# A column group's modulation sum emitted later, and chunk A's mean placed by VectorE's clock

## The chip, the cores and the metric

The kernel runs on one core of a Trainium2 chip. The metric is the device time of one execution in microseconds (us). The core's engines are TensorE (PE in the profile: matmuls; PEld is its loading of weights), VectorE (DVE), ScalarE (ACT), GpSimd (POOL) and SyncE (SP, whose queue issues most transfers). Each engine works through its own program in order; semaphores hold an instruction back until what it reads is there.

## The reference

A trunk of two layers on a sequence of 1024 tokens with D = 1024 channels. Layer 0 mixes tokens by a causal Conformer convolution, layer 1 by a multi-scale pool; each is followed by a SwiGLU feed-forward of width 2816. Every sub-layer is an RMSNorm, then a shift and scale, the sub-layer, a gate and the residual add. Shift, scale and gate come from one conditioning vector c. What matters here is the modulation and layer 0's convolution:

```python
c_act = jax.nn.silu(c)
for i in range(DEPTH):
    mod = c_act @ ada_w[i] + ada_b[i]
    sh_m, sc_m, g_m, sh_f, sc_f, g_f = jnp.split(mod, N_ADA, axis=-1)
    h = modulate(rms_norm(x, norm_mix_g[i]), sh_m, sc_m)
    ...
    x = x + (1.0 + g_m)[:, None, :] * y
    h = modulate(rms_norm(x, norm_ffn_g[i]), sh_f, sc_f)
    y = swiglu_ffn(h, ffn_w_gate[i], ffn_w_up[i], ffn_w_down[i])
    x = x + (1.0 + g_f)[:, None, :] * y

def conformer_conv(h, w1, b1, w_dw, b_dw, ln_g, ln_b, w2, b2):
    u = h @ w1 + b1
    a, g = jnp.split(u, 2, axis=-1)
    u = a * jax.nn.sigmoid(g)
    u = causal_depthwise_conv(u, w_dw, width=31) + b_dw
    u = jax.nn.silu(layer_norm(u, ln_g, ln_b))
    return u @ w2 + b2
```

(`causal_depthwise_conv` stands for the long call of the convolution; `ada_w[i]` makes six groups of D columns, numbered 0 to 5 in the order of the split.)

## The kernel before

Channels lie on the 128 partitions, tokens along the free axis. The sequence is worked in two chunks of 512 tokens, A and B. D is cut into 8 blocks of 128 channels. Every product is made of three matmuls of 128 x 512 (`products`, L485), from the high and low halves of a weight and of an activation; the weights come from DRAM as f32 (`raw`) and are split into halves (`w`) on ScalarE and VectorE.

In layer 0 the names are these. `h` is the normed and modulated input, in a high and a low half for each block. `a` and `g` are the two halves of the pointwise product (`conv_in`, L713); u = (a + bias) times the sigmoid `t` of g. The depthwise convolution has 31 taps: VectorE adds up taps in `ca`, ScalarE and GpSimd share others as products `pr` that GpSimd adds up in `pa`, and for two of the blocks TensorE does all or part of them as `tap` products (`pe_taps`, L749). Then comes the layer norm over channels with silu (`layer_norm_silu`, L849): `acc`, the sum over the eight blocks, goes through a product with ones (`mean`), which is taken off u; the squares are added up and give `var`, VectorE takes its inverse root in small steps (`col`), and TensorE spreads it (`rstd`). Then u times rstd, silu on ScalarE, and the result `v` in two halves, which the products `y` (`conv_out`, L912) read. In layer 0's feed-forward the products are called `p`, then `dn`, which reads `g` again.

The columns of the modulation are made by `ada_columns` (L426), a generator: a load of 128 rows of `ada_w` (`adaw`), four small matmuls into `ada`, eight times for each group. `columns_done` (L449) then copies the sum out on ScalarE, waits a "spread", turns it into columns by small matmuls (`adac`), and adds the bias into `mod` on VectorE.

What sets the order: TensorE's program is written in the order in which the Python code emits its matmuls. All else, from norms to taps and modulation columns, is held in tasks, generators that are moved on between units of eight products by `pace` (L220). For that the code keeps a modelled clock of each engine (`clock`, with the keys PE, V, G and S), advanced by prices at every instruction that it emits (`Engine`, L104). A task says with each `yield` what it waits for, and `Task.step` (L250) turns this into a time `until` before which the task isn't moved on, measured against the modelled clock of TensorE. For an urgent task a word such as "stats" gives the clock at its last mark, plus the VectorE work emitted since, plus the fixed delay of `DELAY` (L66: 2.75 for "stats", 3.0 for "spread"). For others it gives the later of the clocks of VectorE and ScalarE, plus the delay. The order of VectorE, ScalarE and GpSimd then follows from a scheduler that takes the emitted instructions by priority.

`finish` (L232) forces given tasks to their end, with `until` left out of account, and moves the modelled clock of TensorE along with those of VectorE and GpSimd. In the main schedule it is called twice ahead of `ada_second`: for the first columns and for the taps of chunk A (L1589 and L1590).

Of the kernel before, what the change touches and what calls it, by code (L numbers as in the profile page):

```python
# [18 lines left out]
S = 1024  # L19
KT = D // P  # L20
# [3 lines left out]
CW = 31  # L24
# [28 lines left out]
PE_TAPS = {6: 15, 7: CW}  # L53
# [74 lines left out]
def trunk(ctx, tc, xT, c, vec, ada, adan, w1f, w1, wdg, w2, wgu, wdn, wpl, out):  # L128
    nc = tc.nc
    ctx.enter_context(tc.manual_schedule(engines={mybir.EngineType.PE}))  # L130
    clock = {"PE": 0.0, "V": 0.0, "G": 0.0, "S": 0.0}
# [9 lines left out]
    def matmul(out, lhsT, rhs, start, stop, more=False):  # L141
        n = out.shape[-1]
        clock["PE"] += n / 2400 * (1 if rhs.dtype == F32R else 4) + 0.0025
        last_mm[0] = nc.tensor.matmul(out, lhsT, rhs, start=start, stop=stop, skip_group_check=more).ins.name  # L144
# [47 lines left out]
    def nm(s):  # L192
        uid[0] += 1
        return f"{s}_{uid[0]}"
# [5 lines left out]
    forced = [False]  # L200
# [3 lines left out]
    def step(t, e):  # L204
        behind[0] = not t.urgent
        before = {k: engines[k].spent for k in "VG"}
        with tc.high_priority(offset=0 if t.urgent else -LATER):
            moved = t.step(e)
        behind[0] = False
        if V_.spent > before["V"] and getattr(t, "dots", False):  # L210
            recent.append(V_.last.ins)
            del recent[:-RECENT]
        if V_.spent > before["V"] and isinstance(t, Taps) and t.ch.i:
            beside.append(V_.last.ins)
            del beside[:-BESIDE]
        for k in "VG":
            clock[k] += (stretch[0] - 1) * (engines[k].spent - before[k])
        return moved
# [10 lines left out]
                if clock[e] < clock["PE"] + ahead:  # L229
                    moved = any(step(t, e) for t in list(tasks)) or moved  # L230

    def finish(*these):  # L232
        forced[0] = True
        for t in these:
            while not t.done:
                e = "V" if clock["V"] <= clock["G"] else "G"
                o = "VG"[e == "V"]
                if not any(step(q, e) for q in [t] + tasks) and not any(step(q, o) for q in [t] + tasks):
                    raise RuntimeError("nothing moves")
                clock["PE"] = max(clock["PE"], min(clock["V"], clock["G"]))  # L240
        forced[0] = False

    class Task:

# [5 lines left out]
        def step(self, e):  # L250
            if e != "V" or self.done or clock["PE"] < self.until and not forced[0]:
                return False
            try:
                if self.mark is None:
                    self.mark = clock["PE"] - V_.spent
                said = next(self.gen)
                if said == "wait":
                    return False
                if said in LOAD:
                    self.until = clock["PE"] + LOAD[said]  # L260
                elif said == "root":
                    self.until, self.mark = clock["PE"] + DELAY[said], None
                elif said is not None:
                    self.until = (self.mark + V_.spent if self.urgent else max(clock["V"], clock["S"])) + (DELAY if self.urgent or not lax[0] else DELAY_BEHIND)[said]
                    self.mark = None
            except StopIteration:
                self.done = True
                tasks.remove(self)
            return True
# [23 lines left out]
    def bank(name):  # L293
        return ps.tile([P, 512], F32, tag="mm", name=nm(name))
# [15 lines left out]
    def temp(n, name="t", bufs=0):  # L310
        t = tmp.tile([P, TMPW], F32, tag=name if bufs else "t", name=nm(name), bufs=bufs or 4)
        return t[:, :n]
# [46 lines left out]
    def V(name, j, n=1):  # L359
        b = _COLS[name] + j  # L360
        return vecs[:, b : b + n]
# [45 lines left out]
    def ada_gains(l, j, k, n, eng):  # L407
        b = (l * 6 + j) * KT + k
        m = mod[:, b : b + n]
        lk = l * KT + k  # L410
        if j in (1, 4):
            dst, g = (scale_m, "norm_mix_g") if j == 1 else (scale_f, "norm_ffn_g")
            dst = dst[:, lk : lk + n]
            eng.tensor_scalar(dst, m, 1.0, None, op0=ADD)
            eng.tensor_tensor(dst, dst, V(g, lk, n), op=MUL)
        elif j in (2, 5):
            dst = (gate_m if j == 2 else gate_f)[:, lk : lk + n]
            eng.tensor_scalar(dst, m, 1.0, None, op0=ADD)
            if j == 2 and l == 0:
                eng.tensor_tensor(gate_b, dst, V("conv_b2", k, n), op=MUL)  # L420
            if j == 2 and l % 2 == 1:
                eng.tensor_tensor(dst, dst, V("pool_ls", k, n), op=MUL)
# [26 lines left out]
    def columns_done(j, acc):  # L449

        rows = temp(Q)
        S_.copy(rows, acc[:, :Q])
        yield "spread"
        cols = bank("adac")
        for h in range(2):
            matmul(cols[:, 4 * h : 4 * h + 4], rows[:, h * P : h * P + P], quarters, start=True, stop=True)
        m = mod[:, j * KT : (j + 1) * KT]
        V_.tensor_tensor(m.rearrange("p (q h) -> p q h", h=2), cols[:, :KT].rearrange("p (h q) -> p q h", h=2),
                         V("ada_b", j * KT, KT).rearrange("p (q h) -> p q h", h=2), op=ADD)
        ada_gains(0, j, 0, KT, G_)  # L460
        ada_done.add((0, j))
# [186 lines left out]
    def unit(emit, *weights):  # L648
        units.append((weights, emit))
# [188 lines left out]
    def centred(vs, mean, n):  # L838

        held = temp(n, "ny", 2)  # L840
        S_.copy(held, mean)
        for k in range(KT):
            if k % 3 == 1:
                G_.tensor_tensor(vs[k], vs[k], held, op=SUB)
            else:
                V_.tensor_tensor(vs[k], vs[k], mean, op=SUB)
        yield

    def layer_norm_silu(ch):  # L849

        n = ch.n
        vs = [st["u", ch.i, k][:, HALO:] for k in range(KT)]
        acc = None
        for k in range(1, KT):
            while not (st["taps", ch.i][k - 1] and st["taps", ch.i][k]):
                yield "wait"
            was = vs[0] if k == 1 else acc
            if k == KT - 1 or ch.i and acc is None:
                acc = temp(n, "acc", 2)
            elif acc is None:  # L860
                acc = bank("acc")
            V_.tensor_tensor(acc, was, vs[k], op=ADD)
            yield
        if ch.i:
            calm[0], stretch[0] = True, 1.0
            clock["V"] = clock["G"] = clock["PE"]
        yield "soon" if ch.i else "stats"
        b = bank("mean")
        matmul(b, ones, acc, start=True, stop=True)
        if ch.i == 0:  # L870
            yield from centred(vs, b, n)
        else:
            for k in range(KT):
                V_.tensor_tensor(vs[k], vs[k], b, op=SUB)
                yield
        quiet[0] = not ch.i
        acc = yield from sum_sq([vs[k] for k in CENTRED], n)
        quiet[0] = False
        recent.clear()
        if ch.i == 0:  # L880
            for ins in beside:
                tc.add_manual_dep(ins, V_.last.ins.name, edge, reason="behind the sums")
            recent.extend(beside[2:])
            beside.clear()
        rstd = yield from mean_rsqrt(acc, n, when="settled" if ch.i else "stats", early=not ch.i)
        S_.activation(tmp.tile([P, 16], F32, tag="col0", name=nm("col"), bufs=1)[:, 0:1], acc[:, 0:1], AF.Silu)
        hv = [pair(f"h{ch.i}", "v") for _ in range(KT)]
        sws = []

        def low(k):  # L890
            (V_ if ch.i else (G_, V_)[k % 2]).tensor_tensor(hv[k][1], sws[k], hv[k][0].bitcast(F32), op=SUB)

        for k in range(KT):
            V_.tensor_tensor(vs[k], vs[k], rstd, op=MUL)
            sw = temp(n)
            sws.append(sw)
            S_.activation(sw, vs[k], AF.Silu, bias=V("conv_ln_b", k), scale=V("conv_ln_g", k))
            hi, lo = hv[k]
            if ch.i == 0 and k % 2 == 0:
                V_.tensor_copy(hi, sw)  # L900
            else:
                S_.copy(hi, sw)
            if ch.i == 0:
                low(k)
            elif k:
                low(k - 1)
            yield
        if ch.i:
            low(KT - 1)
        st["v", ch.i] = hv  # L910
# [623 lines left out]
    T = {}  # L1534
# [52 lines left out]
            unit(*u)  # L1587
    unit(lambda take: held.__setitem__(0, True))
    unit(lambda take: finish(T["ada", 0]))  # L1589
    unit(lambda take: finish(*(T["taps", 0, p] for p in range(KT) if PE_TAPS.get(p, 0) < CW)))  # L1590

    def ada_second(take):
        T["ada_f"] = Task(ada_columns((4, 5)), False, 0)
# [187 lines left out]
```

## Time and profile before

| | us |
|---|---|
| median of three runs | 1742.52 |
| the three runs | 1741.44, 1743.19, 1742.52 |
| the profiled execution, its own time | 1743.91 |
| its span | 1741.8 |
| idle time of DVE ahead of `x<-dn` in the span | 97.9 |
| granted clock of PE, mean | 0.994 |

The page of the profile gives the busy time of each engine, the chain of work that ended last (followed back from the last instruction), the groups of instructions by line, and the waits of an engine by what released it. A timeline row gives the start in us, the time of the run of instructions, the engine, the line, the operation, output<-inputs, shapes and count, and in brackets the idle time just ahead of it and what ended it. L122 is the line at which the helper issues every instruction of VectorE, ScalarE and GpSimd, and L144 that of every matmul, so rows are told apart by names. A row of the windows table gives the stretch, its length, TensorE's busy time and its instructions, TensorE's granted clock (1.00 is full), the DMA engines' busy share, and GB/s.

### The profile page before, as it was taken

Reading aid. Unit: us, or ns where it says so; the run is one execution under the profiler, and the core shown is the slowest. Engines: PE = TensorE matmul, PEld = TensorE weight load, DVE = VectorE, ACT = ScalarE, POOL = GpSimd, SP = SyncE. Lnnn points to the kernel's source line nnn. Section 1 sums busy time; section 2 is a strip of 40 time slices with the busy share of each in tenths; the row PEclk is TensorE's granted clock in tenths of the full one; section 3 lists DMA queues with packets and bytes.
Section 4 is the critical chain, followed back from the end, with each engine's and each line's share of the span. In section 5 each row is a group of like instructions: output and inputs, shape, how many; then the busy total and the mean of one; then the engine's idle time right before and its main releaser. Section 6 shows DMA issues by size and latency. Waiting matters only on the chain.

```text
span 1741.8 us, 21683 instructions
## 1 busy us (share of the span) xinstructions
PE 1705.0 (98%) x7746; PEld 1388.1 (80%) x7746; DVE 1305.9 (75%) x1878; ACT 788.9 (45%) x1080; POOL 465.9 (27%) x547
## 2 busy tenths in 40 slices
PE   6999999999998999999999999999999999999997
PEld 5777777778886888888888888888788888888887
DVE  8889898899668788877665987858767667555655
ACT  3669687876555233333223337457333333222213
POOL 4587767795001112221110201111111111000001
PEclk9999999999999999999999999999999999999999
DMA  7858987836776888877886837887777674656461
GB/s 286 289 168 224 228 230 201 213 100 208 242 236 183 268 257 266 279 245 253 319 271 214 265 114 221 238 294 209 231 216 208 174 217 139 265 199 208 165 237 61
DMA packets 111309, 384.91 MB, mean 221 GB/s; under 512 B 12129, under 2 KB 14305, under 8 KB 111202
## 3 DMA queue, kind: packets, MB, share of 16 engines
q1 hardware_dynamic: 74832, 256.11, 41.6%
q0 software_dynamic: 35280, 126.37, 29.3%
q8 instruction: 61, 1.00, 0.2%
q10 hardware_dynamic: 1090, 1.05, 0.2%
q14 instruction: 46, 0.38, 0.1%
HBM read 315.33 MB, written 63.96 MB: 218 GB/s over the span
## 4 chain that ended last, share of the span: by engine, by line
PE 87%; DVE 5%; DMA 3%; issue 2%; POOL 1%; ACT 1%; SPq 0%; DVEq 0%; POOLq 0%; ACTq 0%
PE dn L144 26%; PE a L144 22%; PE e L144 12%; PE p L144 11%; PE y L144 6%; PE g L144 3%; PE first L144 2%; PE tap L144 2%; DMA adaw<-in_adan_dram 1%; DMA gd<-g 1%; POOL pa L122 1%; PE ada L144 1%; DVE t L122 1%; PE var L144 1%; DVE adaw L122 1%
## 5 line engine op out<-in xcount | busy, mean ns | idle before, releaser
L122 ACT CAST w<-raw 128x1024 fp32r<-128x1024 f32 x269 | 281.7, 1050 | 489.4 <-PE dn L144 225.1
L144 PE MATMUL dn<-g,w 128*128 128x512 f32 (+1 forms) x2184 | 484.7, 383 | 2.1 <-DVE g L122 1.0
L144 PEld LDWEIGHTS dn<-g,w 128*128 128x128 f32 x2184 | 399.7, 188 | 82.6 <-DVE g L122 1.3
L122 DVE TENSOR_TENSOR w<-raw,w 128x1024 fp32r<-128x1024 f32 x195 | 241.7, 1243 | 63.7 <-ACT w L122 62.2
L144 PE MATMUL a<-n,w 128*128 128x512 f32 x1056 | 249.6, 392 | 4.0 <-DVE r L122 2.7
L144 PE MATMUL p<-h,w 128*128 128x512 f32 x1056 | 244.2, 390 | 0.9 <-DVE h L122 0.7
L144 PEld LDWEIGHTS a<-n,w 128*128 128x128 f32 x1056 | 198.9, 189 | 47.8 <-DVE r L122 3.7
L122 POOL TENSOR_TENSOR pa<-pa,pr 128x512 f32<-128x512 f32 x160 | 227.8, 1509 | 24.8 <-ACT pr L122 18.5
L144 PEld LDWEIGHTS p<-h,w 128*128 128x128 f32 x1056 | 197.3, 188 | 43.8 <-DVE h L122 1.5
L122 DVE SCALAR_TENSOR_TENSOR x<-dn,gains,x 128x512 f32<-128x512 f32 (+1 forms) x200 | 138.5, 725 | 98.1 <-PE dn L144 97.9
L122 DVE SCALAR_TENSOR_TENSOR ca<-u,vecs,ca 128x512 f32<-128x512 f32 x245 | 169.7, 745 | 0.5
L144 PE MATMUL a<-t,w 128*128 128x512 f32 x528 | 126.3, 395 | 3.9 <-ACT w L122 1.9
L144 PE MATMUL e<-b,w 128*128 128x512 f32 x528 | 123.4, 389 | 0.6 <-DVE r L122 0.6
L144 PE MATMUL e<-t,w 128*128 128x512 f32 x528 | 123.2, 389 | 0.0
L144 PEld LDWEIGHTS a<-t,w 128*128 128x128 f32 x528 | 100.5, 191 | 26.4 <-DVE w L122 3.1
L122 ACT ACTIVATE pr<-u,vecs 128x512 f32<-128x512 f32 x160 | 108.2, 716 | 25.1 <-POOL pa L122 17.9
L144 PEld LDWEIGHTS e<-b,w 128*128 128x128 f32 x528 | 99.0, 188 | 21.6 <-DVE r L122 1.0
L144 PEld LDWEIGHTS e<-t,w 128*128 128x128 f32 x528 | 99.1, 188 | 20.6
L1090 POOL DMA_DIRECT2D raw<-in_wgu_dram x42 | 37.2, 885 | 290.4 <-DMA raw<-in_wgu_dram 75.4
L161 POOL DMA_DIRECT2D gd<-g x76 | 46.3, 611 | 198.9 <-DVE g L122 198.5
L144 PE MATMUL y<-v,w 128*128 128x512 f32 x384 | 89.2, 391 | 0.5 <-DVE v L122 0.5
L144 PEld LDWEIGHTS y<-v,w 128*128 128x128 f32 x384 | 71.5, 188 | 17.5 <-issue 1.6
(164 smaller groups left out, 1982.9 us busy)
## 6 DMA issues: line engine op xcount, KB each, us to landing
raw<-in_wgu_dram SPq DMA_DIRECT2D x132, 512.0 KB, 4.8
raw<-in_wdn_dram SPq DMA_DIRECT2D x88, 512.0 KB, 7.0
gd<-g POOLq DMA_DIRECT2D x76, 512.0 KB, 6.9
g<-gd SPq DMA_DIRECT2D x76, 512.0 KB, 6.0
adaw<-in_ada_dram POOLq DMA_DIRECT2D x48, 512.0 KB, 7.0
raw<-in_wgu_dram POOLq DMA_DIRECT2D x42, 512.0 KB, 7.2
raw<-in_w_dram SPq DMA_DIRECT2D x36, 512.0 KB, 5.7
adaw<-in_adan_dram SPq DMA_DIRECT2D x32, 512.0 KB, 5.8
```

The source lines that it names most:

```text
L122: self.last = self.order(getattr(self.eng, name)(out, *args, **kw))
L144: last_mm[0] = nc.tensor.matmul(out, lhsT, rhs, start=start, stop=stop, skip_group_check=more).ins.name
L161: return order(nc.gpsimd.dma_start(*a))
L1090: d = order(nc.gpsimd.dma_start(w[i], wgu[l, fp, src], accum_op=ADD))
```

## The change

Three things change. `columns_done` yields a second "spread" between the adac matmuls and the add into `mod`. In `layer_norm_silu` chunk A's mean is placed by a new word, "mean": `until` becomes the later of the modelled clocks of VectorE and ScalarE, plus 1.0, where "stats" had added the VectorE work since the mark and 2.75. And the `finish` for the taps of chunk A puts the modelled clock of TensorE back to where it was.

```diff
-    def finish(*these):
-        forced[0] = True
+    def finish(*these, aside=False):
+        forced[0], was = True, clock["PE"]
...
                 clock["PE"] = max(clock["PE"], min(clock["V"], clock["G"]))
         forced[0] = False
+        if aside:
+            clock["PE"] = was
...
                     self.until = clock["PE"] + LOAD[said]
+                elif said == "mean":
+                    self.until, self.mark = max(clock["V"], clock["S"]) + 1.0, None
...
             matmul(cols[:, 4 * h : 4 * h + 4], rows[:, h * P : h * P + P], quarters, start=True, stop=True)
+        yield "spread"
         m = mod[:, j * KT : (j + 1) * KT]
...
-        yield "soon" if ch.i else "stats"
+        yield "soon" if ch.i else "mean"
...
-    unit(lambda take: finish(*(T["taps", 0, p] for p in range(KT) if PE_TAPS.get(p, 0) < CW)))
+    unit(lambda take: finish(*(T["taps", 0, p] for p in range(KT) if PE_TAPS.get(p, 0) < CW), aside=True))
```

TensorE's program differs only in its first 565 rows or so (up to some 430 us), with the same matmuls in another order; VectorE's, ScalarE's and GpSimd's differ further on only in the numbers of buffers. One tap product goes from VectorE to GpSimd's sum, and ScalarE loads its table of functions two times more.

The first place is TensorE's program at the mean of chunk A, where the units `a_1941`, `g_1942` and the next are products of chunk B with `h`. Before:

```order
L144 MATMUL a_1941<-h_774,w_1735 128x512 x3
L144 MATMUL ada_1976<-adaw_1930,ccols 32x256 x4
L144 MATMUL mean_1983<-acc_1928,ones 128x512
L144 MATMUL g_1942<-h_767,w_1795 128x512 x3
L144 MATMUL g_1942<-h_768,w_1795 128x512 x3
L144 MATMUL g_1942<-h_769,w_1795 128x512 x3
```

And with the change:

```order
L144 MATMUL a_1941<-h_774,w_1728 128x512 x3
L144 MATMUL ada_1976<-adaw_1930,ccols 32x256 x4
L144 MATMUL g_1942<-h_767,w_1794 128x512 x3
L144 MATMUL g_1942<-h_768,w_1794 128x512 x3
L144 MATMUL g_1942<-h_769,w_1794 128x512 x3
L144 MATMUL g_1942<-h_770,w_1794 128x512 x3
L144 MATMUL mean_2006<-acc_1928,ones 128x512
L144 MATMUL g_1942<-h_771,w_1794 128x512 x3
```

The mean stands four products, 12 matmuls, further back. The var and rstd rows that follow from it move by 12 matmuls each as well (from ahead of a unit to behind its fourth product), while the first row of `y` is the 305th of TensorE's program in both.

The second place is VectorE's program at the add into `mod` of the group j = 3, amid the taps of chunk A's block `u_687`. Before:

```order
L122 SCALAR_TENSOR_TENSOR ca_1557<-u_687,vecs,ca_1557 128x512
L122 TENSOR_TENSOR mod<-adac_1758,vecs 128x8
L122 SCALAR_TENSOR_TENSOR ca_1525<-u_687,vecs,ca_1525 128x512
L122 SCALAR_TENSOR_TENSOR ca_1557<-u_687,vecs,ca_1557 128x512
L122 SCALAR_TENSOR_TENSOR ca_1525<-u_687,vecs,ca_1525 128x512
L122 SCALAR_TENSOR_TENSOR ca_1557<-u_687,vecs,ca_1557 128x512 x3
L122 TENSOR_TENSOR ca_1525<-pa_1495,ca_1525 128x512
L122 SCALAR_TENSOR_TENSOR ca_1557<-u_687,vecs,ca_1557 128x512
```

And with the change:

```order
L122 SCALAR_TENSOR_TENSOR ca_1509<-u_687,vecs,ca_1509 128x512
L122 SCALAR_TENSOR_TENSOR ca_1571<-u_687,vecs,ca_1571 128x512 x2
L122 TENSOR_TENSOR ca_1509<-pa_1487,ca_1509 128x512
L122 SCALAR_TENSOR_TENSOR ca_1571<-u_687,vecs,ca_1571 128x512
L122 TENSOR_TENSOR mod<-adac_1779,vecs 128x8
L122 SCALAR_TENSOR_TENSOR u_687<-u_687,vecs,ca_1509 128x512
```

The add into `mod` has moved behind the sum with `pa` and behind six more taps of this block (the numbers of the buffers differ, the block is the same).

The third place is ScalarE's program ahead of the first silu of chunk A (the ACTIVATE that reads `u_638`, the first block). Before:

```order
L122 CAST w_2242<-raw_2240 128x1024
L122 ACTIVATE w_2242<-raw_2240 128x1024
L122 ACTIVATE t_2192<-u_638,vecs 128x512
L122 ACTIVATE t_2197<-u_638,vecs 128x512
L122 ACTIVATE t_2202<-u_649,vecs 128x512
```

And with the change:

```order
L122 CAST w_2197<-raw_2195 128x1024
L122 ACTIVATE w_2197<-raw_2195 128x1024
L122 ACT_TABLE_LOAD
L122 ACTIVATE t_2186<-g_2079,vecs 128x512
L122 ACT_TABLE_LOAD
L122 ACTIVATE t_2233<-u_638,vecs 128x512
L122 ACTIVATE t_2238<-u_638,vecs 128x512
```

A sigmoid (`t_2186`, of chunk B's unit `g_2079`) with a table load on either side now stands ahead of the silus; before, that sigmoid came behind all eight of them. On VectorE the u that reads it stands ahead of the products with rstd, with two taps behind it.

## The prediction

> **What bounds the kernel now.** I read the busy shares first, then the chain that ended last, then TensorE's waits, and then the timeline of the stretch that the change reorders.
>
> ```profile
> span 1741.8 us, 21683 instructions
> PE 1705.0 (98%) x7746; PEld 1388.1 (80%) x7746; DVE 1305.9 (75%) x1878; ACT 788.9 (45%) x1080; POOL 465.9 (27%) x547
> PE 87%; DVE 5%; DMA 3%; issue 2%; POOL 1%; ACT 1%; SPq 0%; DVEq 0%; POOLq 0%; ACTq 0%
> 460.43 43.52 PE y L144 x192
> ```
>
> TensorE is busy for 98% of the span and holds 87% of the chain. The chain's run of 192 matmuls in 43.52 us gives the price of one full matmul: 0.2267 us. The change neither adds nor removes a matmul, so it can only win or lose in TensorE's idle time and in its clock. TensorE runs in program order, and its order is the same again from about 430 us on. So the question is which waits before that point go, and which appear. By TensorE's waits and its timeline, these stand in the changed stretch:
>
> ```profile
> 173.04 0.64 PE L144 MATMUL ada<-adaw,ccols 128*32 128x256 f32 x8 [0.84 <-DMA adaw<-in_adan_dram]
> 246.18 5.29 PE L144 MATMUL y<-v,w 128*128 128x512 f32 x22
> 251.94 0.73 PE L144 MATMUL y<-v,w 128*128 128x512 f32 x2 [0.47 <-DVE v L122]
> 312.82 1.66 PE L144 MATMUL p<-h,w 128*128 128x512 f32 x6 [0.34 <-DVE h L122]
> 314.80 0.74 PE L144 MATMUL p<-h,w 128*128 128x512 f32 x2 [0.32 <-DVE h L122]
> 365.93 0.50 PE L144 MATMUL dn<-g,w 128*128 128x512 f32 x1 [0.44 <-ACT g L122]
> 367.41 13.65 PE L144 MATMUL dn<-g,w 128*128 128x512 f32 x59 [0.98 <-DVE g L122]
> ```
>
> Together 0.84 + 0.47 + 0.34 + 0.32 + 0.44 + 0.98 = 3.39 us. That is all that can be won by better placing: 0.19% of the span. A loss has no such lid.
>
> **The later modulation sum.** The add into `mod` held VectorE up once in this stretch:
>
> ```profile
> DVE mod L122 <- PE adac L144: 2.5, 1, 2.5
> 187.99 0.17 DVE L122 TENSOR_TENSOR mod<-adac,vecs 128x8 f32<-128x8 f32 x1 [2.55 <-PE adac L144]
> 209.63 1.50 DVE L122 TENSOR_TENSOR acc<-acc,u 128x512 f32<-128x512 f32 x2
> 212.36 1.13 PE L144 MATMUL mean<-acc,ones 128*128 128x512 f32 x2
> ```
>
> In the changed order six more tap instructions and a sum stand ahead of that add. The adac matmuls stand two rows later on TensorE, but the taps ahead of the add take about as long as the stall (six taps at 0.67 us and one sum, some 4.6 us), so the 2.55 us go. This pays nothing: chunk A's sum `acc` was ready at 209.63 + 1.50 = 211.13, before the mean's slot at 212.36. TensorE does not wait there now, and the mean's slot, not `acc`, starts the norm. If instead VectorE still stalled in full, the same 1.23 us of slack and the later slot would cover it up to 3.95 us. So 0, with bounds 0 to 0. The `ada` groups keep their number. Each is issued eight products (one unit) later than before or at a neighbouring place; two of them leave the y phase for the p phase, 0.57 us each from one phase to the other, 0 in the sum. Their loads on SyncE's queue keep the same issuing places as far as I can see. The wait of 0.84 us at 173.04 I leave as it is: bounds −0.84 (it vanishes) and +1.14, the longest wait of this kind, in a row quoted below; I take the one that the same place had.
>
> **The mean's place.** Before, the mean was issued ahead of a unit; now it stands after four products of it. Each product is three matmuls, so 12 × 0.2267 = 2.72 us later on TensorE. The variance and the rstd matmuls, each placed from the one ahead, stand 12 matmuls later too. The first y product stands in the same row of TensorE's order, with the same work ahead of it. So the path mean → centring → variance → rstd → silu → v starts 2.72 us later, and its end is where TensorE already waited 0.47 us, so there is no slack in front of it: v came at 251.89 and TensorE resumed at 251.94.
>
> What can shorten or lengthen this path is VectorE and ScalarE work between rstd and the last v:
>
> ```profile
> 228.49 5.35 DVE L122 SCALAR_TENSOR_TENSOR ca<-u,vecs,ca 128x512 f32<-128x512 f32 x8
> 234.01 4.87 DVE L122 TENSOR_TENSOR u<-u,rstd 128x512 f32<-128x512 f32 x8 [0.17 <-PE rstd L144]
> 248.57 2.72 DVE L122 SCALAR_TENSOR_TENSOR ca<-u,vecs,ca 128x512 f32<-128x512 f32 x4
> 251.21 0.68 DVE L122 TENSOR_TENSOR v<-t,v 128x512 fp32r<-128x512 f32 x1
> 224.64 0.67 ACT L122 ACTIVATE t<-g,vecs 128x512 f32<-128x512 f32 x1
> 225.32 1.28 ACT L122 ACT_TABLE_LOAD   x1
> 233.31 1.06 ACT L122 ACTIVATE w<-raw 128x1024 fp32r<-128x1024 f32 x1
> 234.80 2.23 ACT L122 ACTIVATE t<-u,vecs 128x512 f32<-128x512 f32 x3 [0.43 <-DVE u L122]
> ```
>
> A tap instruction is 5.35 / 8 = 0.67 us. Between the rstd products and the last v, ten of them stand before and eight now: −2 × 0.67 = −1.34. Against this, ahead of the rstd products VectorE now has `u<-a,vecs,t`, which needs a sigmoid on ScalarE, and that brings a table load before and one behind it, ahead of the first silu. From the end of the weight's cast (233.31 + 1.06 = 234.37) I count 1.28 + 0.67 to 236.32; VectorE then does the u (0.75) and two taps (1.34) and starts the rstd products at 238.4 instead of 234.0: +4.4. The ends are therefore 2.72 − 1.34 = +1.4 (table loads hidden by the shift, fewer taps pay in full) and +4.4 (sigmoid in the way, fewer taps pay nothing, as the silus pace the v). With both it is 4.4 − 1.34 = +3.1. I take the plain shift, **+2.72**, which lies between and near the middle.
>
> **What goes later.** For chunk A's next norm VectorE now makes three t ahead of the first low half of h, and the third low half (the one waited for at 312.82) comes one instruction, some 0.67 us, earlier; ahead of the fourth (314.80) stand as many as before. So the first p wait goes and the second stays or grows into its place: of 0.66 I take about half, **−0.3** (bounds −0.66 and 0). At the dn wait ScalarE has one product fewer ahead of the last cast of g, and VectorE one tap (0.67) more ahead of its last g: I take ScalarE's wait of 0.44 as gone and VectorE's as it was, **−0.4** (bounds −1.42, both gone, and +0.67). If I am wrong nothing covers these; TensorE stands still for each of them. The one tap product that the change hands from VectorE to GpSimd, 0.67 us of VectorE's time, lies beside other work on both.
>
> **The sum.** +2.72 − 0.3 − 0.4 = +2.0. The profiled execution took 1743.91 us, span 1741.8 and 2.1 around it; with +2.0 it would be 1745.9. It lies 1.39 above the median of the three runs, 1742.52, so for a median I forecast 1742.52 + 2.0 = **1744.5**.
>
> **Rivals.**
>
> *The clock falls (slower).* TensorE's granted clock has fallen in this kernel after short gaps:
>
> ```profile
> 94.16 0.64 PE L144 MATMUL ada<-adaw,ccols 128*32 128x256 f32 x8 [1.14 <-DMA adaw<-in_adan_dram]
> 95.64 7.34 PE L144 MATMUL a<-h,w 128*128 128x512 f32 x24
> 160.22 5.74 PE L144 MATMUL a<-h,w 128*128 128x512 f32 x24
> 92.00:95.00 3.00, 1.86 (x16) 1.00 1.02 411
> 95.00:100.00 5.00, 5.00 (x19) 0.66 1.05 309
> 172.00:176.00 4.00, 3.16 (x20) 1.00 1.05 297
> 364.00:368.00 4.00, 2.58 (x11) 1.00 0.29 95
> 368.00:372.00 4.00, 4.00 (x19) 1.00 0.09 38
> ```
>
> Behind a gap of 1.14 us the clock (the fourth number of a window row) was 0.66, and 24 matmuls took 7.34 instead of 5.74 us: 1.60 us. Behind 0.84 us at 173 and behind 0.44 and 0.98 us at 366 it stayed at 1.00. The y wait grows from 0.47 to about 3.2 us; if it falls in one or two pieces of over about 1.1 us, from which this rival decides, the price is 1.60 once or twice, and the time is 1744.5 + 1.60 = 1746.1, or with the p and dn waits not won (+0.7) 1746.8. [...] Here the trace does not agree: the drop at 95 came behind 1.14 us; so the measurement keeps this rival alive, at 0.28.
>
> *The path absorbs it (faster).* There is filler on VectorE all along the path from rstd to v, and the eight taps ahead of the rstd products need not all be done in the waiting. If the later start only eats filler, the y wait stays near 0.5, and the waits at `ada`, p and dn may go: −0.3 − 0.4 gives 1741.8, with both p and dn waits and the `ada` wait gone −0.66 − 1.42 − 0.84 = −2.9, so 1739.6; all seven rows gone gives 1742.52 − 3.39 = 1739.1. For it speaks that 3.29 us of VectorE's time ahead of the centring was idle:
>
> ```profile
> 214.41 3.08 DVE L122 TENSOR_TENSOR u<-u,mean 128x512 f32<-128x512 f32 x5 [3.29 <-ACT ny L122]
> ```
>
> Against it: that idle time grows with the later mean. Chance 0.20, about 1740.8.
>
> *No effect.* The slot of the mean moves, but v and the waits come out as before, the lost slot made up by the two taps fewer and the p and dn waits: 1742.5. Chance 0.10.
>
> **How the numbers follow.** Forecast 0.42, the falling clock 0.28, absorbed 0.20, no effect 0.10. About 0.2%, 3.5 us, is what a measurement of this kernel tells from no change: below 1739.0 is faster, above 1746.0 slower. The forecast lies mostly in "same", with its upper end (+4.4 − 0.3 + 0.67, so 1747.3) in slower: of 0.42 I put 0.34 and 0.08, the falling clock half and half (0.14 each), absorbed 0.08 faster (1739.1 stands at the bound, and the three runs spread by 1.75) and 0.12 same, no effect all same. Faster 0.08, same 0.70, slower 0.22. The range for 8 in 10 runs from 1740.0, which leaves out the better half of the absorbed case, to 1747.3, which takes in the forecast's upper end and one drop of the clock.
>
> **What would show it.** Right: in the changed profile the mean's row 2.7 us later against its unit, no stall on `mod` in VectorE's waits, rstd products about 3 to 4 us later, a y wait on v of 2 to 4 us in one to four pieces, one p wait instead of two near 315. The clock rival shows as a granted clock under 0.9 within 5 us of the y unit and 24 matmuls in over 6 us. The forecast is wrong if the y wait stays under 1 us, if the `ada` loads come late again at another place (a wait on the DMA of over 1 us), or if VectorE's taps push a wait into the phase from 260 to 430 us that I do not see.

## The result, and the profile after

Slower: 1747.21 us (1745.79 to 1750.42, seven runs) against 1741.99 (1738.77 to 1743.19, seven runs), a ratio of 1.0034 [1.0025, 1.0044]. The direction of the forecast was right and its size was not: +2.0 us was forecast, +5.2 came (by the interval, 4.4 to 7.7). The time lies just under the upper end of the range, 1747.3. The profiled execution took 1747.59 us, with a span of 1745.7.

TensorE's waits in the changed kernel (in total, times, longest, in us), of those in the changed stretch:

```profile
PE y L144 <- DVE v L122: 2.9, 4, 0.9
PE p L144 <- ACT t L122: 1.1, 1, 1.1
PE dn L144 <- DVE g L122: 1.0, 1, 1.0
PE y L144 <- POOL v L122: 0.9, 1, 0.9
PE p L144 <- DVE h L122: 0.4, 1, 0.4
```

The y unit waits 3.8 us for v instead of 0.5; a wait of p on ScalarE is new; ScalarE's 0.4 at dn is gone. TensorE's timeline of the first y unit:

```profile
243.23 1.46 PE L144 MATMUL y<-v,w 128*128 128x512 f32 x4
245.52 1.67 PE L144 MATMUL y<-v,w 128*128 128x512 f32 x6 [0.83 <-DVE v L122]
247.44 0.73 PE L144 MATMUL y<-v,w 128*128 128x512 f32 x2 [0.25 <-DVE v L122]
249.09 0.50 PE L144 MATMUL y<-v,w 128*128 128x512 f32 x1 [0.92 <-DVE v L122]
250.48 1.34 PE L144 MATMUL y<-v,w 128*128 128x512 f32 x3 [0.88 <-POOL v L122]
252.68 3.78 PE L144 MATMUL y<-v,w 128*128 128x512 f32 x8 [0.86 <-DVE v L122]
256.39 1.08 PE L144 MATMUL ada<-adaw,ccols 128*32 128x256 f32 x8
257.40 5.85 PE L144 MATMUL y<-v,w 128*128 128x512 f32 x24
```

Five waits, together 3.74 us. Behind the last of them eight matmuls take 3.78 us, 0.47 each, where one took 0.2267 before. The windows of TensorE (stretch, length, busy time, clock, DMA share, GB/s) show the granted clock at half there:

```profile
244.00:248.00 4.00, 2.92 (x11) 1.00 0.99 209
248.00:252.00 4.00, 2.01 (x5) 0.86 1.04 268
252.00:256.00 4.00, 3.32 (x8) 0.50 0.22 44
256.00:260.00 4.00, 4.00 (x21) 0.79 0.37 114
```

From the first y matmul to that of the second unit it is 257.40 − 243.23 = 14.17 us; before it was 253.17 − 246.18 = 6.99. That is **+7.2 us** in one place. ScalarE's timeline ahead of it shows what was late:

```profile
231.39 1.28 ACT L122 ACT_TABLE_LOAD   x1
232.69 0.69 ACT L122 ACTIVATE t<-g,vecs 128x512 f32<-128x512 f32 x1
236.15 1.28 ACT L122 ACT_TABLE_LOAD   x1 [2.77 <-DVE u L122]
237.44 1.52 ACT L122 ACTIVATE t<-u,vecs 128x512 f32<-128x512 f32 x2
```

The sigmoid has a table load ahead of it, and behind it a second one, which did not start until the first product u times rstd was there (2.77 us idle). So the first silu is late by VectorE's delay and by the load. VectorE's timeline:

```profile
188.18 0.70 DVE L122 TENSOR_TENSOR ca<-pa,ca 128x512 f32<-128x512 f32 x1 [2.62 <-POOL pa L122]
205.84 1.50 DVE L122 TENSOR_TENSOR acc<-acc,u 128x512 f32<-128x512 f32 x2
213.87 3.08 DVE L122 TENSOR_TENSOR u<-u,mean 128x512 f32<-128x512 f32 x5 [6.53 <-ACT ny L122]
233.41 0.75 DVE L122 SCALAR_TENSOR_TENSOR u<-a,vecs,t 128x512 f32<-128x512 f32 x1 [1.16 <-ACT t L122]
235.39 4.86 DVE L122 TENSOR_TENSOR u<-u,rstd 128x512 f32<-128x512 f32 x8
240.17 1.40 DVE L122 SCALAR_TENSOR_TENSOR ca<-u,vecs,ca 128x512 f32<-128x512 f32 x2
242.16 3.30 DVE L122 TENSOR_TENSOR v<-t,v 128x512 fp32r<-128x512 f32 x1
245.39 1.40 DVE L122 SCALAR_TENSOR_TENSOR ca<-u,vecs,ca 128x512 f32<-128x512 f32 x2
247.31 1.40 DVE L122 SCALAR_TENSOR_TENSOR ca<-u,vecs,ca 128x512 f32<-128x512 f32 x2
248.96 1.40 DVE L122 SCALAR_TENSOR_TENSOR ca<-u,vecs,ca 128x512 f32<-128x512 f32 x2
250.62 1.40 DVE L122 SCALAR_TENSOR_TENSOR ca<-u,vecs,ca 128x512 f32<-128x512 f32 x2
251.94 2.37 DVE L122 TENSOR_TENSOR v<-t,v 128x512 fp32r<-128x512 f32 x2
```

The stall on `mod` is gone from VectorE, and 2.62 us on GpSimd's `pa` stand in its place. Chunk A's sum ends at 207.34, and VectorE then idles 6.53 us ahead of the centring, where it was 3.29. Behind the products with rstd (the rows shown are not all) five pairs of taps, ten in all, stand ahead of the last two low halves of v, which end at 254.31.

The two profiled spans differ by 3.9 us only, less than the y unit. At the start of y TensorE is 2.95 us ahead of before (243.23 against 246.18). Of this, 1.6 us is the clock, which fell at about 95 us in the profiled execution of before (0.57 in 96 to 100 us, and 24 matmuls in 7.34 us) and not in this one (1.00, and 5.71 us), and 0.5 us is a shorter wait of `ada` on its load (0.84 in before, 0.34 here). The experiments show that this fall of the clock comes and goes with the execution.

### The profile page after: what moved, and what is told of

It is laid out like the page before. It is cut to its first block, busy times and chain, and to the rows that moved or that the text cites. A ratio compares the mean times of both kernels' runs of the same rounds, so it can differ in the third digit from the quotient of the medians.

```text
span 1745.7 us, 21679 instructions
## 1 busy us (share of the span) xinstructions
PE 1707.3 (98%) x7746; PEld 1388.9 (80%) x7746; DVE 1305.0 (75%) x1877; ACT 792.3 (45%) x1083; POOL 469.9 (27%) x548
## 4 chain that ended last, share of the span: by engine, by line
PE 86%; DVE 5%; issue 3%; DMA 3%; ACT 2%; POOL 1%; SPq 0%; DVEq 0%; POOLq 0%; ACTq 0%
PE dn L144 26%; PE a L144 22%; PE e L144 12%; PE p L144 11%; PE y L144 6%; PE first L144 3%; PE g L144 2%; PE tap L144 2%; DMA adaw<-in_adan_dram 1%; DVE ca L122 1%; DMA gd<-g 1%; DVE t L122 1%; PE ada L144 1%; PE var L144 1%; DVE u L122 1%
## 5 line engine op out<-in xcount | busy, mean ns | idle before, releaser
L122 POOL TENSOR_TENSOR pa<-pa,pr 128x512 f32<-128x512 f32 x161 | 231.5, 1513 | 17.3 <-ACT pr L122 14.9
```

What stands on the lines that cost most here:

```text
L122: self.last = self.order(getattr(self.eng, name)(out, *args, **kw))
```

## The experiments

Twelve kernels, each timed in five rounds beside the kernel before, whose medians in the four batches were 1741.56, 1740.4, 1741.22 and 1741.6. Ratios are to it, with a 95% interval. Such an interval is 3.0 to 4.7 us wide; so the time tells the change from the kernel before, but not the parts of the loss from each other, and those are read from one profiled execution of each kernel.

Theory 1: the distance between the mean and the first y product, and what stands between them, make the loss. Theory 2: the later sum into `mod` and the moved `ada` groups do.

**mean_back.** The changed kernel, with one number:

```diff
-                    self.until, self.mark = max(clock["V"], clock["S"]) + 1.0, None
+                    self.until, self.mark = max(clock["V"], clock["S"]) + 0.0, None
```

> The changed kernel with the mean of chunk A at 0.0 instead of 1.0 behind the clocks, which puts it back ahead of its unit (row 257 of TensorE's program, as before); the later sum into mod stays. Theory 1, the mean's place costs the 5.2 us: 1741 to 1742.5, y waits under 1 us in the first y unit, granted clock 1.00 there. Theory 2, the later sum and the moved ada groups cost it: 1745 to 1747.5, with the ScalarE wait of about 1.1 us near 335 us still there.

Measured: 1741.02, 0.9996 [0.9986, 1.0005]. TensorE's timeline:

```profile
242.10 5.29 PE L144 MATMUL y<-v,w 128*128 128x512 f32 x22
247.87 0.73 PE L144 MATMUL y<-v,w 128*128 128x512 f32 x2 [0.48 <-DVE v L122]
```

The y unit is that of before. With this number every engine has the order of instructions that the second "spread" alone gives, and `aside` moves no instruction. So the later sum is worth nothing that can be measured, either way. The new wait of 1.10 us at p is here too, so it comes with the later sum's order and not with the mean.

**mean_only.** The kernel before with the new word for the mean, and nothing else of the change:

```diff
-        yield "soon" if ch.i else "stats"
+        yield "soon" if ch.i else "mean"
```

> The kernel before with the mean's new place alone (row 261), the sum into mod as before. Theory 1 (the mean's place): 1746 to 1748, y waits of 3 to 4 us and a granted clock of 0.5 to 0.8 behind them. Theory 2 (the later sum): 1741.5 to 1742.5.

Measured: 1747.86, 1.004 [1.0027, 1.0053]; y waits of 3.5 us, clock 0.51 in 256 to 260. TensorE's waits at p and dn are those of before (0.32 and 0.31, 0.40 and 0.99), and the new one at p is missing. Theory 2 falls with this pair: the mean's place makes the whole loss.

**u_behind_silu.** The changed kernel; one unit's u (`HELD_U` names it: chunk B's unit 3, that of `g_2079`) is kept and issued at the end of chunk A's norm.

```diff
-                conv_glu(ch, p, *b, fine < 4)
+                if (ch.i, p) in HELD_U:
+                    held_u.append((ch, p, *b))
+                else:
+                    conv_glu(ch, p, *b, fine < 4)
...
         st["v", ch.i] = hv
+        if not ch.i:
+            while held_u:
+                conv_glu(*held_u.pop(0))
```

> The changed kernel with the sigmoid and u of chunk B's unit (t_2186, u_1939) emitted behind chunk A's silus, so that no second table load stands ahead of the first silu; the mean stays at its new place. Theory 1a, the table load and the sigmoid make v late: the first silu starts about 2.6 us earlier, y waits fall from 3.7 to 1 or 1.5 us, the clock stays at 1.00, time 1741.5 to 1743. Theory 1b, the later mean alone makes v late: y waits stay over 3 us, time 1746 to 1748.

Measured: 1745.35, 1.0023 [1.0015, 1.0032]. Its lines stand one number further on:

```profile
245.35 3.25 PE L145 MATMUL y<-v,w 128*128 128x512 f32 x13
249.88 0.96 PE L145 MATMUL y<-v,w 128*128 128x512 f32 x3 [1.28 <-POOL v L123]
252.09 2.10 PE L145 MATMUL y<-v,w 128*128 128x512 f32 x8 [1.25 <-DVE v L123]
248.00:252.00 4.00, 1.57 (x6) 1.00 0.98 267
252.00:256.00 4.00, 3.91 (x22) 1.00 0.61 118
```

Between the two expectations: the clock stays at 1.00, but 2.53 us of waits remain. So the sigmoid is one part of the cause, and the distance, which is as in the changed kernel, another. The y unit is 4.83 us shorter than in the changed kernel and the median 1.9 us only; the intervals of the two ratios overlap, and I did not find where the rest stays.

**y_filled.** The changed kernel with ten matmuls of zeros in the first y unit (`zeros` is a tile that GpSimd sets to 0 at the start):

```diff
                         products(b, wt, k, st["v", ch.i][k], k == 0, k == KT - 1)
+                    if ch.i == 0 and ds == (0,) and k in (0, 1, 2, 3, 4):
+                        for _ in range(2):
+                            matmul(bs[0], zeros, st["v", 0][k][0], start=False, stop=False)
+                            clock["PE"] -= 512 / 2400 + 0.0025
```

> The changed kernel with ten more matmuls in the first y unit, two behind each of its first five products, of zeros times v, added into the same sum (they add 0 and change no result); 10 x 0.2267 = 2.27 us, less than the 3.74 us that TensorE waits there. If the granted clock falls because of the gaps: it stays at 1.00 in this unit, the first y unit ends some 3 us earlier, time 1743.5 to 1745. If the clock has nothing to do with the gaps: it falls as before or the fillers cost their own time, 1747 to 1749.5.

Measured: 1745.75, 1.0028 [1.0016, 1.0039]: 1.5 us of median below the changed kernel, which is less than expected and not clear of the noise. The last rows of its y unit and the window there:

```profile
252.24 2.44 PE L144 MATMUL y<-v,w 128*128 128x512 f32 x8 [0.80 <-DVE v L122]
254.61 0.64 PE L144 MATMUL ada<-adaw,ccols 128*32 128x256 f32 x8
252.00:256.00 4.00, 3.70 (x20) 1.00 0.15 29
```

The last eight matmuls take 2.44 us instead of 3.78 and the `ada` group 0.64 instead of 1.08: 1.34 + 0.44 = 1.78 us. That is what the trace gives as the price of the clock, at the end of the unit, where v no longer hides it.

**mean_later** and **mean_earlier.** As mean_back, with 5.0 and with −3.0.

> The changed kernel with 5.0 instead of 1.0: the mean at row 266, a further half unit and an ada group (2.72 + 0.57 us) behind the change's place; var and rstd move along. If the distance sets it: y waits of 6 to 7.5 us in the first y unit instead of 3.7, a clock of 0.5 behind them, 1749.5 to 1752. If the sigmoid ahead of the silus was most of it and is not so placed here: 1745 to 1748.

> The changed kernel with -3.0 instead of 1.0 behind the clocks: the mean stands at row 252 of TensorE's program, nine rows ahead of the change's place and five ahead of the old one. If the distance between mean and first y product sets the y wait: no y wait in the first y unit, but TensorE waits 1 to 2 us at the mean, since chunk A's sum is ready only about 1.4 us after that place; 1740.5 to 1743. If the distance is not what sets it: y waits as with the mean at row 257 (0.5 us) and 1742 to 1744 for the new wait.

Measured: mean_later 1746.0, 1.0034 [1.0022, 1.0046]; mean_earlier 1746.24, 1.0031 [1.0018, 1.0043]. The time of mean_later lies in its second range, but not for the reason given there: the sigmoid and its two loads stand ahead of the silus here too (4.80 us from rstd to the first silu). That of mean_earlier was missed. TensorE's rows, of mean_later first:

```profile
246.03 0.49 PE L144 MATMUL y<-v,w 128*128 128x512 f32 x1 [2.12 <-DVE v L122]
248.71 8.37 PE L144 MATMUL y<-v,w 128*128 128x512 f32 x23 [2.18 <-POOL v L122]
```

And of mean_earlier:

```profile
208.57 1.10 PE L144 MATMUL mean<-acc,ones 128*128 128x512 f32 x2 [1.39 <-DVE acc L122]
245.92 5.74 PE L144 MATMUL y<-v,w 128*128 128x512 f32 x24
252.70 5.73 PE L144 MATMUL y<-v,w 128*128 128x512 f32 x24 [0.46 <-DVE u L122]
```

The later mean costs what the change costs, and not more: the waits are 4.30 us, and the path behind rstd is 2.5 us shorter than in the changed kernel (table below), which makes up for most of the 3.4 us that the distance loses. The earlier mean does away with the y wait, as expected, and pays 1.39 us at the mean, as expected. But it also reorders the rest, chunk B's mean, var and rstd among it (up to some 450 us), and that brings waits of 0.46 us here, 1.19 on VectorE's u at dn and 1.49 on ScalarE's r at p. With the mean's wait they are 4.5 us (1.39 + 0.46 + 1.19 + 1.49); which of them follow from the mean's place alone I did not separate.

**table_twice.** mean_back with one tiny sigmoid behind the small silu that loads the table early and writes `col`:

```diff
+        if ch.i == 0:
+            S_.activation(col[:, 1:2], col[:, 0:1], AF.Sigmoid)
```

> The mean back at row 257 (as in mean_back), with one more tiny sigmoid (128x1, its result read by nobody) on ScalarE behind the small silu that loads the silu's table early; nothing else moves. The first silu then needs a table load of 1.28 us of its own, which cannot start before u times rstd is there. If this load is part of the path to v: y waits of 1.4 to 2.4 us instead of 0.5, 1742 to 1743.5. If it is hidden: y waits of 0.5 us, 1740.5 to 1741.5.

Measured: 1741.27, 1.0005 [0.9995, 1.0014]. The time is that of a hidden load, yet the load is not hidden. ScalarE's timeline, and VectorE's first two low halves of v, of before and then of table_twice:

```profile
235.37 1.28 ACT L122 ACT_TABLE_LOAD   x1 [0.42 <-DVE u L122]
236.66 2.23 ACT L122 ACTIVATE t<-u,vecs 128x512 f32<-128x512 f32 x3
240.79 3.94 DVE L122 TENSOR_TENSOR v<-t,v 128x512 fp32r<-128x512 f32 x2
241.38 2.40 DVE L122 TENSOR_TENSOR v<-t,v 128x512 fp32r<-128x512 f32 x2
```

The load stood ahead of the first silu as foreseen, and the first silu came 3.25 us behind rstd instead of 1.98. Yet the last v came earlier, and the y unit had no wait at all. In before the two low halves that VectorE made beside GpSimd's took 3.94 us; here the pair takes 2.40. A silu that is late by itself is not yet a v that is late.

**table_early.** The changed kernel, u and its sigmoid still ahead, with a tiny silu behind that sigmoid:

```diff
         S_.activation(sg, bg, AF.Sigmoid, bias=V("conv_b1", KT + p))
+        if (ch.i, p) == (1, 3):
+            S_.activation(tmp.tile([P, 16], F32, tag="col0", name=nm("col"), bufs=1)[:, 0:1], sg[:, 0:1], AF.Silu)
```

> The changed kernel (mean at row 261, u and its sigmoid still ahead of the silus) with a tiny silu (128x1, read by nobody) right behind that sigmoid, so that ScalarE loads the silu's table before u times rstd is there; the sigmoid then needs no load of its own either. If the two table loads of 1.28 us make v late: the first silu starts 2 to 2.5 us behind the rstd matmul instead of 4.75, y waits of 2 to 3 us, time 1743.5 to 1745.5. If VectorE's u and taps ahead of the products with rstd make it late: over 4 us as before, 1746.5 to 1748.

Measured: 1744.19, 1.0019 [1.001, 1.0029]. TensorE:

```profile
243.59 3.56 PE L144 MATMUL y<-v,w 128*128 128x512 f32 x13
248.04 0.97 PE L144 MATMUL y<-v,w 128*128 128x512 f32 x3 [0.90 <-POOL v L122]
250.25 2.43 PE L144 MATMUL y<-v,w 128*128 128x512 f32 x8 [1.24 <-DVE v L122]
```

As the first alternative has it. The table of the silu is loaded before u times rstd is there, so the load is off the path; the path is as short as before, the clock stays at 1.00, and the y unit takes 9.59 us instead of 14.17. The median falls by 3.0 us, to a ratio whose interval still overlaps that of the change. What is left, 0.19% or 3.3 us, is clear of no change and near to the distance.

**lows_on_dve** and **lows_on_dve_back.** The changed kernel, and mean_back, each with GpSimd's four low halves of v on VectorE.

```diff
-            (V_ if ch.i else (G_, V_)[k % 2]).tensor_tensor(hv[k][1], sws[k], hv[k][0].bitcast(F32), op=SUB)
+            V_.tensor_tensor(hv[k][1], sws[k], hv[k][0].bitcast(F32), op=SUB)
```

> The changed kernel with all eight low halves of v on VectorE (four of them were on GpSimd). In the changed kernel the first low on VectorE took 3.3 us instead of 0.68 while GpSimd made one too. If that meeting of the two engines lengthens the path to v: no low over 1 us, rstd to last v 19 to 20.5 us instead of 21.6, 1745 to 1746.5. If four more instructions on VectorE cost what the meeting did: 21.5 us or more, 1747 to 1748.5.

> The mean back at row 257 and all eight low halves of v on VectorE. If the meeting of VectorE and GpSimd lengthens the path: rstd to last v 17 to 18.5 us instead of 19.1, no y wait, 1740 to 1741.5, so at most 0.5 us better than mean_back. If VectorE becomes the limit: y waits of 1 us or more, 1742 to 1743.5.

Measured: 1749.31, 1.0047 [1.0034, 1.0061], and 1746.8, 1.003 [1.0021, 1.004]. Both paths became shorter than with GpSimd's help (18.99 instead of 21.63 us, 18.60 instead of 19.08), and both times longer, above what either alternative expected. In the first the y unit still waits 3.44 us, as the distance is that of the change, and the clock falls there again (0.58 in 256 to 260). In the second, TensorE's timeline has this row:

```profile
251.60 5.73 PE L144 MATMUL y<-v,w 128*128 128x512 f32 x24 [1.70 <-DVE u L122]
```

The second y unit waits for VectorE's u, which reads an older product (I take it that `y` gets that product's buffer of the pool of six, which no run separates); and p waits 3.82 us for ScalarE. So the four low halves were better off on GpSimd; I take it that VectorE's other work pays for them, which no run separates.

**gap_filled** and **table_ahead_of_p.** Two tries at beating both kernels from mean_back: 13 matmuls of zeros in the waits at 555 us (7 ahead of the first product of that unit, 6 ahead of its third matmul), and the tiny silu of table_early behind the sigmoid of chunk B's last unit instead.

```diff
+                if (l, fp, name) == (0, 1, "t2"):
...
+                    for _ in range(7):
+                        matmul(b, zeros, h[j][0], start=True, stop=False, more=True)
                     matmul(b, wt[:, 0, wk], h[j][0], start=True, stop=False, more=True)
                     matmul(b, wt[:, 0, wk], h[j][1], start=False, stop=False, more=True)
+                    for _ in range(6):
+                        matmul(b, zeros, h[j][0], start=False, stop=False, more=True)
                     matmul(b, wt[:, 1, wk], h[j][0], start=False, stop=False, more=True)
...
-        if (ch.i, p) == (1, 3):
+        if (ch.i, p) == (1, 5):
```

> The mean back at row 257, and 13 matmuls of zeros (7 ahead of the product that waits for ScalarE's weights at about 555 us, 6 ahead of the one that waits for VectorE's low half; they add 0): 1.59 and 1.36 us into waits of 2 to 3 and 1.5 to 2 us. If short gaps drop the clock: the granted clock stays at 1.00 from 552 to 568 us instead of 0.55 to 0.6, and the time falls by 2 to 3 us, to 1738 to 1739.5. If the clock does not follow the gaps: 1741 to 1743.

> The mean back at row 257, with a tiny silu (128x1, read by nobody) on ScalarE behind the sigmoid of chunk B's last unit, so that the silu's table is loaded some 20 us before the first silu of p; nothing else moves. In mean_back TensorE waits 1.10 us at about 326 us for that silu, right behind a table load of 1.28 us. If that load makes the wait: no wait there, 1.1 us less than mean_back, 1739.5 to 1740.5, below both kernels by about 1 us, which is inside the noise of a median. If the silu is late for another reason: the wait of 1.1 us stays, 1741.

Measured: 1741.91, 1.001 [1.0002, 1.0019], and 1744.11, 1.0011 [1.0001, 1.002]. In gap_filled the clock fell all the same, earlier (in before it was 0.56 in 560 to 564 us and 0.58 in 564 to 568), and the fillers took their time:

```profile
552.00:556.00 4.00, 2.17 (x10) 0.99 1.02 350
556.00:560.00 4.00, 4.00 (x12) 0.59 1.05 319
```

In table_ahead_of_p the wait at p is half as long, the time is above both alternatives, and the next wait is for a load that comes late:

```profile
328.59 3.02 PE L144 MATMUL p<-h,w 128*128 128x512 f32 x12 [0.56 <-ACT t L122]
339.12 0.64 PE L144 MATMUL ada<-adaw,ccols 128*32 128x256 f32 x8 [1.27 <-DMA adaw<-in_adan_dram]
```

Neither beats the kernel before; no version here does.

**The path in numbers.** From the timelines of the profiled executions, in us: from the mean's start to where TensorE is free for y; from the rstd matmul's start to that of the first silu, and to the end of the last v; the waits inside the first y unit; and from where TensorE is free for y to the start of the second unit.

| kernel | mean to y | rstd to first silu | rstd to last v | y waits | y unit | ratio |
|---|---|---|---|---|---|---|
| before | 33.82 | 1.98 | 19.07 | 0.47 | 6.99 | 1 |
| mean_back | 33.82 | 1.98 | 19.08 | 0.48 | 7.00 | 0.9996 |
| table_twice | 33.82 | 3.25 | 17.67 | 0 | 6.24 | 1.0005 |
| after | 31.05 | 4.75 | 21.63 | 3.74 | 14.17 | 1.0034 |
| mean_only | 31.05 | 4.76 | 21.61 | 3.47 | 14.16 | 1.004 |
| table_early | 31.05 | 2.23 | 18.86 | 2.14 | 9.59 | 1.0019 |
| u_behind_silu | 31.05 | 1.87 | 17.83 | 2.53 | 9.34 | 1.0023 |
| y_filled | 31.05 | 4.75 | 21.64 | 2.03 | 12.37 | 1.0028 |
| lows_on_dve | 31.05 | 4.76 | 18.99 | 3.44 | 12.13 | 1.0047 |
| mean_later | 27.65 | 4.80 | 19.16 | 4.30 | 13.67 | 1.0034 |

The change's +7.18 us of y unit split into three: 33.82 − 31.05 = 2.77 of distance, 21.63 − 19.07 = 2.56 of path, and the rest, 1.85, the clock (y_filled: 14.17 − 12.37 = 1.80).

## Why the prediction was right or wrong

- **The bound** held: the stretch named is the one that moved, and TensorE's waits and clock there account for the loss. The y unit's +7.18 with the later waits at p and dn (−0.28, +1.10, −0.43, below) is +7.6, at the upper end of the measured 4.4 to 7.7 us.
- **The later modulation sum at 0** held (mean_back). The stall on `mod` went and nothing came of it: GpSimd's `pa` made VectorE wait 2.62 us at the same place, and chunk A's sum, ready 1.23 us ahead of the mean before and 4.85 us now (212.19 − 207.34), had no one waiting for it.
- **The mean's place, +2.72**, was right as a distance: 2.77 measured, and some 3 us of time left in table_early, where the path is as before.
- **The path from rstd to v was the step that failed.** The prediction took it as unchanged, with the sigmoid and two fewer taps cancelling; it grew by 2.56 us. The two fewer taps, −1.34, do not exist: ten taps stand between the products with rstd and the last v in both kernels (VectorE's rows above), so nothing stood against the sigmoid. The sigmoid's own way was read well: from the start of its table load to the first product with rstd the prediction counted 4.03 us (234.37 to 238.4) and 4.00 came (231.39 to 235.39), which puts that product 1.51 us later against the rstd matmul (2.70 instead of 1.19). The second table load was named but not priced: it stood behind u times rstd, and the first silu starts 2.05 us behind the first product instead of 0.79, so 1.26 more. Together the first silu is 2.77 us late, and only 0.21 of it came back up to the last v (first silu to last v: 17.09 before, 16.88 after).
- **The upper end** of the mean's place and the path was +4.4, which holds the sigmoid's way and not the second load; 2.77 + 2.56 = 5.33 lies above it. That 1747.21 is still under 1747.3 is luck: that end was to take in either the longer path or one fall of the clock, and both came.
- **The clock, the slower rival**, came true as well, at 0.50 of full in 252 to 256 us and a cost of 1.80 us (1.60 was its price), against a chance of 0.28, which rested on one fall, the one behind 1.14 us at 95 us. Its condition, a single gap of over about 1.1 us, was wrong: here five gaps of at most 0.92 us did it, and two of 1.28 and 1.25 us in u_behind_silu did not. It was treated as an alternative to the forecast, and it came on top of it: without the path's 2.56 us the clock stayed up in the profiled execution of table_early. What makes it fall stays open.
- **Later waits.** The dn term, −0.4, measured −0.43 (0.44 + 0.98 before, 0.99 after). The p term, −0.3, was right for the waits that it names, two of which became one of 0.38 (−0.28). It missed a new one of 1.10 us some 20 us later, on ScalarE's first silu of p behind a table load; with that load placed earlier 0.56 us of wait is left (table_ahead_of_p). All of these come with the later sum's order: mean_back has them and mean_only has not. The `ada` wait at 173, kept at 0.84, was 0.34 in the changed kernel and absent in mean_only, whose program is that of before up to there, so it changes with the execution.

## What to carry to other kernels

Count the distance of a statistic in TensorE's program from its first reader: here that reader already waited, and 12 matmuls of delay took 2.77 us of the distance, and 3.3 us of time were left in table_early with the path as short as before, though the inputs were ready 4.85 us ahead of the mean. Before moving something on such a path, look at which function tables the activation engine will load between its steps: here a load of 1.28 us that stood behind a data wait was on the path (the first silu 4.75 us behind rstd), and a tiny activation placed earlier took it off (2.23 us in table_early). Count the instructions between two points in both programs before a term rests on their number. Price a fall of the clock on top of a forecast and not only in its place: here it added 1.8 us to waits of 3.74 us. The lengths of the waits did not tell whether it falls (it did at five of at most 0.92 us, and did not at 1.28 and 1.25 us in u_behind_silu).

## What the runs showed of the hardware that I had not expected

In the traces of four kernels a table load came only behind the data wait of the activation that needed it: in the changed kernel ScalarE idled 2.77 us for u, and only then loaded for 1.28 us; in table_twice it idled 0.42 us ahead of such a load, in mean_later 1.96 us and in mean_earlier 4.79 us.

The clock at 95 us falls in one execution and not in another. The gap there is an `ada` group waiting for its load. Behind it the clock in 96 to 100 us was 0.53 to 0.72 in before, mean_only, u_behind_silu, table_twice, mean_earlier, gap_filled and lows_on_dve, and 1.00 in the seven others. In those that fell the wait was 0.93 to 2.13 us and TensorE was busy for 1.87 to 3.08 us of 92 to 96 us; in those that did not, 0.66 to 1.06 us and 2.99 to 3.34 us. So the two groups overlap. mean_back and table_twice have the same program of TensorE, and fell on different sides (1.00 and 0.57).

VectorE's low halves of v, 0.68 us alone, took up to 3.30 us when GpSimd worked on low halves at the same time (the changed kernel at 242.16, with two of GpSimd's from 242.38 on in 2.54 us); with all eight on VectorE (lows_on_dve) eight took 5.14 us, 0.64 each. So in these runs the path's length went with where the two fell on each other. This fits the earlier v behind a later silu in table_twice: the pair of low halves is 1.54 us shorter there (3.94 and 2.40), the path 1.40.
